# Latent attention with a written order on TensorE: keys and queries projected one head ahead, projections set between the transposition and its use

## The chip, the cores and the metric

One core of a Trainium2 chip runs the program. Its engines are TensorE (PE; its weight loads are listed apart as PEld), VectorE (DVE), ScalarE (ACT), GpSimd (POOL) and SyncE (SP), which in this kernel issues most of the DMAs. The metric is the time on the device of one execution, in microseconds (us); smaller is better. A kernel's time is the median of three runs here.

## The reference

A trunk of two layers over 512 tokens of width 1024. The first layer mixes tokens with a gated linear recurrence (HGRN2), the second with latent attention (MLA). Around each mixer stand two half-step SwiGLU blocks of inner width 2816, and at the end of a layer a gated per-layer embedding. The change touches the attention of the second layer alone:

```python
def _mla_mixer(h, positions, k_nope, k_rope, v, w_dq, q_norm, w_uq, w_out):
    c_q = _rmsnorm(h @ w_dq, q_norm)                      # 512 wide latent query
    q = (c_q @ w_uq).reshape(bsz, seq, B_HEADS, B_NOPE + B_ROPE)
    q_nope, q_rope = jnp.split(q, [B_NOPE], axis=-1)      # 128 and 64 wide, 16 heads
    q_rope = _rope(q_rope, positions)
    ...
        s = (jnp.einsum('bqhd,bkhd->bhqk', qn, k_nope)
             + jnp.einsum('bqhd,bkd->bhqk', qr, k_rope)).astype(jnp.float32) * scale
        s = jnp.where(mask[None, None], s, -jnp.inf)      # causal
        pr = jax.nn.softmax(s, axis=-1).astype(v.dtype)
        return jnp.einsum('bhqk,bkhd->bqhd', pr, v)
    ...
    return o @ w_out
```

`k_nope` and `v` are projected, head by head, from one normalised latent of width 256 that the first layer left; `k_rope` is one rotated key shared by all heads.

## The kernel before

**Numbers in two halves.** Every product is made of three passes in a reduced float type: a tensor is split into a rounded high half and the remainder, and `mm3` multiplies high by high (L151), low by high and high by low into the same accumulation. A split is a copy on ACT (`hi`, L166) and a subtraction on DVE (`lo`, L167). A matmul of `mm3` cannot start before its halves exist, and the second and third passes need the low halves, which come last.

**The stream of weights.** All weights come in one sequence of tiles of 128 by 1024, each eight blocks of 128 by 128, in the order in which TensorE uses them. A tile passes through three stages: a DMA into `raw` (five buffers, issued by SP), a cast on ACT into `whi` (L129, three buffers), a subtraction on DVE into `wlo` (L130, three buffers). The cast of a tile waits until TensorE has done with the tile three places earlier, whose `whi` buffer it takes. `block()` hands out the next block.

**PSUM.** Four banks named `mm` take the projections (`chain`), four named `aux` the scores, the transposed probabilities and the weighted sums.

**The attention**, `mla`, does for each of 16 heads: `scores`, which projects the head's key from the two blocks of the shared latent and its query from the four blocks of the query latent, splits both, and computes four rows of tiles, row i having 128(i+1) columns, then the softmax of each row: masked maximum on DVE (L1142), the scaled negative maximum (L1146), exponential with its sum on ACT (L1149), reciprocal on DVE (L1151), multiplication on POOL (L1152); `weigh`, which transposes the ten tiles of probabilities (L1163), splits the three banks (`ph` on ACT, L1167, and `pl` on DVE, L1168), multiplies by the values and splits the result; and `project`, which multiplies the weighted values of two heads by half of the output weights and adds four results into x (L1182). `rope(group)` makes the rotated queries of four heads: two chains on TensorE, eight operations on ACT and DVE, two splits, and sixteen DMAs (`qr`, L1099) issued by SP. `values(p)` makes the values of two heads. The loop calls scores(h), then weigh(h-1), then for most heads a project; the rope of the next group at h = 3, 7 and 11 and the values of the next pair at odd h.

**Who sets the order.** Outside of stretches under `tc.manual_schedule`, a planner orders the instructions of each engine by a simulated time and by priority; `soon(n)` raises the priority of what is written in it (`FETCH_OFF`, 200, for the stream; `EV_OFF`, 400). Before the change the planner orders every engine in `mla`. In the SwiGLU blocks the order is the written one on all engines. Each engine works through its own list in order: an instruction that waits holds back what stands behind it in the list. The weight stream's tiles are ordered by a list on the host (`_stream`) that has to match the order of use.

Of the kernel before, what the change touches and what calls it, by code (L numbers as in the profile page):

```python
# [9 lines left out]
F32 = mybir.dt.float32  # L10
# [47 lines left out]
def kernel(  # L58
# [1008 lines left out]
    def mla(xg, stats, cn, krope, sin, cos, post):  # L1067
# [13 lines left out]
        def rope(group):  # L1081
            pa, pb = chain(cq), chain(cq)
            qa, qb, ta, tb = (slot("rt") for _ in range(4))
            act.copy(qa, pa)
            act.copy(qb, pb)
            dve.tensor_tensor(out=ta, in0=qa, in1=cos, op=ALU.mult)
            dve.tensor_tensor(out=tb, in0=qb, in1=sin, op=ALU.mult)
            dve.tensor_tensor(out=ta, in0=ta, in1=tb, op=ALU.subtract)
            h1, l1 = split(ta)
            dve.tensor_tensor(out=qb, in0=qb, in1=cos, op=ALU.mult)  # L1090
            dve.tensor_tensor(out=qa, in0=qa, in1=sin, op=ALU.mult)
            dve.tensor_tensor(out=qb, in0=qb, in1=qa, op=ALU.add)
            h2, l2 = split(qb)
            res = []
            for j in range(4):
                d = slot("qr", F32R)
                s = slice(32 * j, 32 * j + 32)
                for i, src in enumerate((h1, h2, l1, l2)):
                    nc.sync.dma_start(d[32 * i : 32 * i + 32, :].bitcast(F32), src[s, :].bitcast(F32))  # L1099
                res.append(d)  # L1100
            return res

        def values(p):
            w = [block(2) for _ in range(2)]
            tiles = []
            for i in range(2):
                pv = mm_bank()
                for n in range(2):
                    j = 2 * i + n
                    for k in range(2):  # L1110
                        ck = tuple(a[:, j * P : (j + 1) * P] for a in cn[k])
                        mm3(pv[:, 256 * n : 256 * n + 256], ck, w[k], k == 0, k == 1)
                tiles.append(split(pv, None, "v"))
            return [
# [5 lines left out]
            ]  # L1120
# [35 lines left out]
        def weigh(prob, v):  # L1156
# [8 lines left out]
            for b, w in ((0, 512), (1, 512), (2, 256)):  # L1165
                hi, lo = slot("ph", F32R, "r"), slot("pl", F32R, "r")
                act.copy(hi[:, 0:w], banks[b][:, 0:w])  # L1167
                dve.tensor_tensor(  # L1168
                    out=lo[:, 0:w], in0=banks[b][:, 0:w], in1=hi[:, 0:w].bitcast(F32), op=ALU.subtract
                )  # L1170
                at.append((hi, lo))
            po = aux_bank()
            for j in range(NT):
                b, o = place[j]
                w = T - j * P
                mm3(po[:, j * P :], v[j], (at[b][0][:, o : o + w], at[b][1][:, o : o + w]), j == 0, j == NT - 1)
            return split(po, None, "o")
# [14 lines left out]
        qr, vals = rope(0), values(0)  # L1192
        last = None
        for h in range(B_HEADS):
            ahead = h < B_HEADS - 1
            rotated, value = qr[h % 4], vals[h % 2]
            if h % 4 == 3 and ahead:
                qr = rope(h // 4 + 1)
            if h % 2 == 1 and ahead:
                vals = values(h // 2 + 1)  # L1200
            pr = scores(rotated)
            if last is not None:
                outs.append(weigh(*last))
            last = (pr, value)
            if 2 < h < B_HEADS - 1:
                project((h - 1) // 2 - 1, 1 - h % 2)
        n = B_HEADS - 1
        half = [mm_bank() for _ in range(KC // 2)]
        for ps in half:
            part(ps, (n - 3, n - 2), True, False)  # L1210
        for ps in half:
            part(ps, (n - 1,), False, False)
        outs.append(weigh(*last))
        for m, ps in enumerate(half):
            part(ps, (n,), False, True)
            add(m, ps)
            post(m)
        for m in range(KC // 2, KC):
            ps = mm_bank()
            part(ps, (n - 3, n - 2, n - 1, n), True, True)  # L1220
            add(m, ps)
            post(m)
# [91 lines left out]
def _stream(i):  # L1314
# [65 lines left out]
    turned(0)  # L1380
    valued(0)
    def project(n, part):
        a, b, c = 2 * n * P, (2 * n + 1) * P, (2 * n + 2) * P
        rows = [wo[a:b], wo[b:c]]
        if n < B_HEADS // 2 - 1:
            rows = rows[::-1]
        out.append(_blocks(np.concatenate(rows, axis=0)[:, part * D // 2 : (part + 1) * D // 2]))

    for h in range(B_HEADS):
        ahead = h < B_HEADS - 1  # L1390
        if h % 4 == 3 and ahead:
            turned(h // 4 + 1)
        if h % 2 == 1 and ahead:
            valued(h // 2 + 1)
        out.append(_blocks(wk[:, h, :128]))
        out.append(_blocks(wq[:, h, :128]))
        if 2 < h < B_HEADS - 1:
            project((h - 1) // 2 - 1, 1 - h % 2)
    tail = wo[-4 * P :]
    out.append(_rows(tail[: 2 * P, : D // 2]).reshape(2, KC // 2, P, P).transpose(1, 0, 2, 3).reshape(-1, P, P))  # L1400
    out.append(_rows(tail[2 * P : 3 * P, : D // 2]))
    out.append(_rows(tail[3 * P :, : D // 2]))
    out.append(_blocks(tail[:, D // 2 :]))
# [67 lines left out]
```

## Time and profile before

| | |
|---|---|
| three runs | 2176.10, 2176.32, 2176.52 us; median 2176.32 us |
| profiled execution, its own time | 2175.48 us |
| its span in the profile | 2173.7 us |
| granted TensorE clock, mean | 0.997 |
| PE busy | 2148.8 us, 99% of the span |
| DVE, ACT, POOL busy | 70%, 45%, 14% |
| attention of the second layer (`mla`, loop and entrance) | about 1447 to 1772 us of the span |

The span is that of the hardware profiler; the time of the execution is 1.8 us longer. A line of a group reads: source line, engine, operation, output and inputs with shapes, count, busy us with the mean of one in ns, and the idle time of the engine just before with what ended it. A line of a timeline reads: start, duration, engine, line, operation, and in brackets the idle time before it and its releaser. Line numbers are those of the kernel before (the changed file's lines are a few higher: L1142 becomes L1148, L1149 becomes L1155, L1163 becomes L1169, L1167 becomes L1174).

### The profile page before, as it was taken

Reading aid. Unit: us, or ns where it says so; the run is one execution under the profiler, and the core shown is the slowest. Engines: PE = TensorE matmul, PEld = TensorE weight load, DVE = VectorE, ACT = ScalarE, POOL = GpSimd, SP = SyncE. Lnnn points to the kernel's source line nnn. Section 1 sums busy time; section 2 is a strip of 40 time slices with the busy share of each in tenths; the row PEclk is TensorE's granted clock in tenths of the full one; section 3 lists DMA queues with packets and bytes.
Section 4 is the critical chain, followed back from the end, with each engine's and each line's share of the span. In section 5 each row is a group of like instructions: output and inputs, shape, how many; then the busy total and the mean of one; then the engine's idle time right before and its main releaser. Section 6 shows DMA issues by size and latency. Waiting matters only on the chain.

```text
span 2173.7 us, 32746 instructions
## 1 busy us (share of the span) xinstructions
PE 2148.8 (99%) x13026; PEld 1925.5 (89%) x13026; DVE 1522.3 (70%) x2261; ACT 968.5 (45%) x1374; POOL 313.3 (14%) x428
## 2 busy tenths in 40 slices
PE   8999999999999999999999999999999999999998
PEld 7899998898888899998888989988888888999987
DVE  6776676777786676675767757767676776775765
ACT  6354453223235343344553525446444563443543
POOL 2000001554521000001110000011110110000011
PEclk9999999999999999999999999999999999999999
DMA  5555552211123555552244655423122134654631
GB/s 192 141 157 159 144 163 96 83 69 59 68 69 105 147 159 159 141 160 101 87 119 127 172 146 157 144 91 104 59 85 91 51 105 132 151 164 126 178 104 49
DMA packets 76249, 261.46 MB, mean 120 GB/s; under 512 B 9152, under 2 KB 11328, under 8 KB 76096
## 3 DMA queue, kind: packets, MB, share of 16 engines
q1 hardware_dynamic: 64864, 220.15, 30.4%
q0 software_dynamic: 10368, 37.75, 10.1%
q8 instruction: 102, 1.67, 0.3%
q10 hardware_dynamic: 864, 1.46, 0.2%
q14 instruction: 51, 0.42, 0.1%
HBM read 253.04 MB, written 2.10 MB: 117 GB/s over the span
## 4 chain that ended last, share of the span: by engine, by line
PE 94%; DVE 3%; ACT 1%; issue 1%; DMA 0%; POOL 0%; SPq 0%; POOLq 0%; DVEq 0%; ACTq 0%
PE aux L314 19%; PE mm L151 18%; PE mm L152 18%; PE mm L153 17%; PE mm L314 14%; PE aux L152 1%; PE aux L153 1%; PE aux L723 1%; PE aux L151 1%; PE aux L1163 1%; PE aux L1138 0%; PE aux L1137 0%; ACT whi L304 0%; PE aux L214 0%; DVE wlo L305 0%
## 5 line engine op out<-in xcount | busy, mean ns | idle before, releaser
L151 PE MATMUL mm<-hi,whi 128*128 128x512 f32 x1656 | 647.1, 393 | 8.5 <-ACT whi L1252 5.6
L152 PE MATMUL mm<-lo,whi 128*128 128x512 f32 x1656 | 647.2, 391 | 1.5 <-DVE lo L380 0.9
L153 PE MATMUL mm<-hi,wlo 128*128 128x512 f32 x1656 | 646.1, 390 | 0.0
L305 DVE TENSOR_TENSOR wlo<-raw,whi 128x1024 fp32r<-128x1024 f32 x340 | 425.3, 1251 | 220.6 <-ACT whi L304 217.5
L304 ACT CAST whi<-raw 128x1024 fp32r<-128x1024 f32 x340 | 355.2, 1046 | 288.3 <-PE mm L152 163.5
L151 PEld LDWEIGHTS mm<-hi,whi 128*128 128x128 f32 x1656 | 311.3, 188 | 72.2 <-ACT whi L1252 5.6
L152 PEld LDWEIGHTS mm<-lo,whi 128*128 128x128 f32 x1656 | 311.7, 188 | 64.1 <-DVE lo L380 2.2
L153 PEld LDWEIGHTS mm<-hi,wlo 128*128 128x128 f32 x1656 | 311.5, 188 | 63.4
L314 PE MATMUL aux<-hi,whi 128*128 128x256 f32 x1152 | 328.1, 285 | 2.5 <-ACT mm L465 2.5
L314 PE MATMUL aux<-hi,wlo 128*128 128x256 f32 x1152 | 326.8, 284 | 0.2 <-DVE wlo L300 0.2
L314 PE MATMUL aux<-lo,whi 128*128 128x256 f32 x1152 | 326.5, 283 | 0.0
L314 PE MATMUL mm<-lo,whi 128*128 128x256 f32 x864 | 244.5, 283 | 0.0
L314 PE MATMUL mm<-hi,whi 128*128 128x256 f32 x864 | 244.5, 283 | 0.0
L314 PE MATMUL mm<-hi,wlo 128*128 128x256 f32 x864 | 244.4, 283 | 0.0
L314 PEld LDWEIGHTS aux<-hi,whi 128*128 128x128 f32 x1152 | 221.6, 192 | 3.3 <-ACT mm L465 2.7
L314 PEld LDWEIGHTS aux<-hi,wlo 128*128 128x128 f32 x1152 | 221.7, 192 | 0.5 <-DVE wlo L300 0.5
L314 PEld LDWEIGHTS aux<-lo,whi 128*128 128x128 f32 x1152 | 221.6, 192 | 0.5
L288 POOL DMA_DIRECT2D raw<-in_wall x72 | 62.8, 872 | 941.1 <-DMA raw<-in_wall 538.5
L129 ACT CAST whi<-raw 128x1024 fp32r<-128x1024 f32 x95 | 99.8, 1051 | 171.7 <-PE mm L152 113.1
L314 PEld LDWEIGHTS mm<-lo,whi 128*128 128x128 f32 x864 | 165.9, 192 | 0.0
L314 PEld LDWEIGHTS mm<-hi,whi 128*128 128x128 f32 x864 | 165.9, 192 | 0.0
L314 PEld LDWEIGHTS mm<-hi,wlo 128*128 128x128 f32 x864 | 165.9, 192 | 0.0
(248 smaller groups left out, 2883.6 us busy)
## 6 DMA issues: line engine op xcount, KB each, us to landing
raw<-in_wall SPq DMA_DIRECT2D x402, 512.0 KB, 3.3
raw<-in_wall POOLq DMA_DIRECT2D x72, 512.0 KB, 5.8
x<-in_xT SPq DMA_DIRECT2D x8, 256.0 KB, 6.8
qr<-hi SPq DMA_DIRECT2D x32, 64.0 KB, 2.0
qr<-lo SPq DMA_DIRECT2D x32, 64.0 KB, 2.0
out_dram<-o SPq DMA_DIRECT2D x8, 256.0 KB, 2.3
p<-in_pT ACTq DMA_DIRECT2D x4, 256.0 KB, 4.4
raw<-in_wall SPq DMA_DIRECT2D x2, 256.0 KB, 3.6
```

The lines of the kernel that those rows point to most:

```text
L129: act.copy(hi[:, s], raw[:, s])
L151: pe.matmul(out, a[0], b[0], start=first, stop=False)
L152: pe.matmul(out, a[0], b[1], start=False, stop=False)
L153: pe.matmul(out, a[1], b[0], start=False, stop=last)
L288: nc.gpsimd.dma_start(self.raw, wall[self.plus], accum_op=ALU.add)
L304: act.copy(hi, self.raw)
L305: dve.tensor_tensor(out=lo, in0=self.raw, in1=hi.bitcast(F32), op=ALU.subtract)
L314: pe.matmul(o, w[u][:, s], b[i][v], start=first and e + i + n == 0, stop=False, skip_group_check=True)
L723: pe.matmul(sc[:, e * 192 : (e + 1) * 192].rearrange("p (i b n) -> p i b n", i=2, n=3 * m), k[:, j * P : (j + 1) * P], q4[:, :, j * nbt : ...
L1163: pe.transpose(banks[b][:, o : o + P], prob[i][:, j * P : (j + 1) * P], ident)
```

## The change

The loop over the heads now stands under `tc.manual_schedule` for TensorE: TensorE does in `mla`'s loop what is written, in the order in which it is written. The other engines are still ordered by the planner. The key and query of head h+1 are projected (`project_in`) after the scores of head h. `weigh` is taken apart into `turn_over`, the ten transpositions and the split of their banks, and `weigh`, the products. For a head in the middle TensorE does: scores(h), weigh(h-1), key(h+1), query(h+1), turn_over(h), then, where they fall due, the rope of a group (after h = 6 and 10), the values of a pair (after even h from 2 to 12), and a half project (h from 2 to 13). At the beginning the key of head 0, half of the first values, the rope of group 0, the rest of the values of two pairs, the query of head 0 and the key of head 1 come before scores(0); at h = 0 the rope of group 1 stands around the transpositions; nothing stands between the transpositions of head 1 and scores(2). At the end the first half of the output columns collects heads 12 to 14 around the transpositions of the last two heads, and a fifth chain, in an `aux` bank, collects heads 12 to 14 after the last weigh. The splits, the rope's operations and the split of the transposed banks get the priority `EV_OFF`. The number of matmuls, transpositions, weight tiles and DMAs stays the same, and so do the instructions of each engine.

```diff
-        def rope(group):
-            pa, pb = chain(cq), chain(cq)
-            qa, qb, ta, tb = (slot("rt") for _ in range(4))
...
+        def rope(res):
+            pa = chain(cq)
+            yield
+            pb = chain(cq)
+            with soon(EV_OFF):
+                qa, qb, ta, tb = (slot("rt") for _ in range(4))
...
-        def scores(qr):
-            pk = chain(cn)
-            kk = split(pk)
-            pq = chain(cq)
-            qq = split(pq)
+        def project_in(rhs):
+            ps = chain(rhs)
+            with soon(EV_OFF):
+                return split(ps)
+
+        def scores(kk, qq, qr):
...
-        def weigh(prob, v):
+        def turn_over(prob):
...
+            with soon(EV_OFF):
+                for b, w in ((0, 512), (1, 512), (2, 256)):
+                    hi, lo = slot("ph", F32R, "r"), slot("pl", F32R, "r")
+                    act.copy(hi[:, 0:w], banks[b][:, 0:w])
...
+                    at.append((hi, lo))
+            return [tuple(a[:, o : o + T - j * P] for a in at[b]) for j, (b, o) in enumerate(place)]
+
+        def weigh(at, v):
             po = aux_bank()
             for j in range(NT):
...
+                mm3(po[:, j * P :], v[j], at[j], j == 0, j == NT - 1)
+            with soon(EV_OFF):
+                outs.append(split(po, None, "o"))
...
-        qr, vals = rope(0), values(0)
-        last = None
-        for h in range(B_HEADS):
...
+        def tails(h):
+            for ps in half:
+                part(ps, (h,), h == n - 3, h == n)
+
+        with tc.manual_schedule(engines={mybir.EngineType.PE}):
+            kq = {0: [project_in(cn)]}
+            val, rot = [], []
+            vg, rg = values(val), rope(rot)
+            next(vg)
+            next(rg)
+            next(rg)
+            next(vg)
+            next(vg)
+            for _ in values(val):
+                pass
+            kq[0].append(project_in(cq))
+            kq[1] = [project_in(cn)]
+            at = None
+            for h in range(B_HEADS):
+                pr = scores(*kq.pop(h), rot[h])
+                if at is not None:
+                    weigh(at, val[h - 1])
+                if h == 0:
+                    rg = rope(rot)
+                    kq[1].append(project_in(cq))
+                    next(rg)
+                elif h < n:
+                    kq[h + 1] = [project_in(cn), project_in(cq)]
+                else:
+                    tails(n - 2)
+                at = turn_over(pr)
+                if h == 0:
+                    next(rg)
+                elif h == n - 1:
+                    half.extend(mm_bank() for _ in range(KC // 2))
+                    tails(n - 3)
+                elif h == n:
+                    tails(n - 1)
+                if h in (6, 10):
+                    for _ in rope(rot):
+                        pass
+                if h % 2 == 0 and 0 < h < n - 2:
+                    for _ in values(val):
+                        pass
+                if 1 < h < n - 1:
+                    project((h - 2) // 2, h % 2)
+            weigh(at, val[n])
+            fifth = aux_bank()
+            part(fifth, (n - 3, n - 2, n - 1), True, False)
...
@@ -1377,30 +1421,47 @@
...
+    for h in range(B_HEADS):
+        if h == 0:
+            query(1)
+            turned(1)
+        elif h < n:
+            key(h + 1)
+            query(h + 1)
...
```

Three places of the lists show what follows for ACT. First, ACT ahead of the first softmax. In the list before, `hi_13935` and `hi_13958` are the splits of the key and the query of head 0:

```order
L166 CAST hi_13857<-rt_13850 128x512
L166 CAST hi_13864<-rt_13849 128x512
L129 CAST whi_14350<-raw_14348 128x1024
L166 CAST hi_13935<-mm_13928 128x512
L166 CAST hi_13958<-mm_13939 128x512
L166 CAST hi_14063<-mm_14056 128x512
L166 CAST hi_14086<-mm_14067 128x512
```

And now, where `hi_13994` is the split of the query of head 0 and `hi_14005` that of the key of head 1:

```order
L129 CAST whi_14133<-raw_14131 128x1024
L166 CAST hi_13977<-mm_13964 128x512
L166 CAST hi_13900<-rt_13885 128x512
L129 CAST whi_14286<-raw_14284 128x1024
L166 CAST hi_13994<-mm_13981 128x512
L166 CAST hi_14005<-mm_13998 128x512
L1155 ACT_TABLE_LOAD
```

The cast `whi_14286`, whose buffer is that of the tile `whi_13943`, last read by the end of the key projection of head 1, now stands directly ahead of the split of the query of head 0.

Second, ACT at head 1 and scores(2), in the list now (`hi_14273` and `hi_14296` split the key and the query of head 2, the `ph` are the banks of head 1's transposed probabilities, the `P` are the exponentials of head 1):

```order
L1155 ACTIVATE P_14191,t_14192<-P_14191,t_14214,t_13814 128x256
L129 CAST whi_14514<-raw_14512 128x1024
L1155 ACTIVATE P_14190,t_14192<-P_14190,t_14228,t_13814 128x384
L1155 ACTIVATE P_14189,t_14192<-P_14189,t_14242,t_13814 128x512
L1174 CAST ph_14313<-aux_14300 128x512
L166 CAST hi_14273<-mm_14266 128x512
L1174 CAST ph_14317<-aux_14301 128x512
L166 CAST hi_14296<-mm_14277 128x512
L1174 CAST ph_14321<-aux_14302 128x256
```

The splits of head 2's key and query stand between the splits of head 1's transposed banks, and the cast of a weight tile stands between the second and third exponential. In the list before, the splits of head 2's key and query stand ahead of all of head 1's exponentials. DVE at the same place, now (`wlo_14515` is the low half of that tile; L1148 is the masked maximum, whose second row reads its result; `pl` and `lo` are the low halves that belong to the `ph` and `hi` above):

```order
L130 TENSOR_TENSOR wlo_14515<-raw_14512,whi_14514 128x1024
L1157 RECIPROCAL t_14232<-t_14192 128x1
L1148 ISA P_14189,t_14241<-aux_14235,cs 128x512
L1148 ISA t_14241 128x1
L1152 TENSOR_SCALAR t_14242<-t_14241,t_13814 128x1
L1157 RECIPROCAL t_14246<-t_14192 128x1
L1175 TENSOR_TENSOR pl_14314<-aux_14300,ph_14313 128x512
L167 TENSOR_TENSOR lo_14274<-mm_14266,hi_14273 128x512
L1175 TENSOR_TENSOR pl_14318<-aux_14301,ph_14317 128x512
L167 TENSOR_TENSOR lo_14297<-mm_14277,hi_14296 128x512
```

The maximum of the last row of head 1 now stands behind the subtraction of the weight tile.

Third, ACT at head 7, after a rope group, now (`hi_15442` splits the weighted values of head 6, `hi_15453` and `hi_15476` the key and the query of head 8):

```order
L1155 ACTIVATE P_15371,t_15372<-P_15371,t_15394,t_13814 128x256
L166 CAST hi_15442<-aux_15429 128x512
L1155 ACTIVATE P_15370,t_15372<-P_15370,t_15408,t_13814 128x384
L129 CAST whi_15675<-raw_15673 128x1024
L166 CAST hi_15453<-mm_15446 128x512
L1155 ACTIVATE P_15369,t_15372<-P_15369,t_15422,t_13814 128x512
L166 CAST hi_15476<-mm_15457 128x512
```

Before, the list has, at head 7's softmax, the two splits of the projected key and query ahead of the first exponential, since scores(7) made them itself:

```order
L166 CAST hi_15277<-mm_15270 128x512
L166 CAST hi_15300<-mm_15281 128x512
L166 CAST hi_15451<-mm_15444 128x512
L129 CAST whi_15666<-raw_15664 128x1024
L166 CAST hi_15474<-mm_15455 128x512
L1149 ACTIVATE P_15305,t_15307<-P_15305,t_15315,t_13814 128x128
L1149 ACTIVATE P_15306,t_15307<-P_15306,t_15329,t_13814 128x256
```

Now the exponentials of head 7 are mixed with the splits of head 8's key and query and with a weight cast. The rows of POOL are the same as before.

More of the change, by code (lines that the diff above doesn't have):

```diff
@@ L1100, in rope, with values @@
                 res.append(d)
[L1101 to L1103 removed]
+            yield
+        def values(res):
             w = [block(2) for _ in range(2)]
@@ L1190, in part @@
                 mm3(ps, block(), outs[h], first and i == 0, last and i == len(heads) - 1)
-        qr, vals = rope(0), values(0)
-        last = None
-        for h in range(B_HEADS):
[L1195 to L1206, printed above, removed]
@@ L1207, in mla @@
-        n = B_HEADS - 1
[L1208 to L1222, printed above, removed]
+        n = B_HEADS - 1
@@ new lines, in mla @@
+        half = []
+        def tails(h):
[46 more added lines that the diff above has]
+            part(fifth, (n - 3, n - 2, n - 1), True, False)
+            for m, ps in enumerate(half):
+                part(ps, (n,), False, True)
+                add(m, ps)
+                post(m)
+            for m in range(KC // 2, KC):
+                if m == KC // 2:
+                    ps = fifth
+                    part(ps, (n,), False, True)
+                else:
+                    ps = mm_bank()
+                    part(ps, (n - 3, n - 2, n - 1, n), True, True)
+                add(m, ps)
+                post(m)
```

87 lines of the change are left out of this document (45 added, 42 removed).

## The prediction

> **What bounds the kernel now.** I began with the page, for the bound, then cut the attention into windows.
>
> ```profile
> span 2173.7 us, 32746 instructions
> PE 2148.8 (99%) x13026; PEld 1925.5 (89%) x13026; DVE 1522.3 (70%) x2261; ACT 968.5 (45%) x1374; POOL 313.3 (14%) x428
> PE 94%; DVE 3%; ACT 1%; issue 1%; DMA 0%; POOL 0%; SPq 0%; POOLq 0%; DVEq 0%; ACTq 0%
> ```
>
> TensorE is busy for 99% of the span and carries 94% of the chain that ended last. The number of matmuls and their widths does not change, so the change can move only TensorE's waits, and only those of the attention. There the windows give (us, then busy time and count of PE, PEld, DVE, ACT, POOL, the granted clock, DMA share, GB/s):
>
> ```profile
> 1447.00:1462.00 15.00, 15.00 (x81) 12.86 (x80) 10.88 (x15) 8.51 (x13) 0.00 (x0) 1.00 0.21 71
> 1462.00:1478.00 16.00, 15.28 (x86) 13.24 (x85) 14.05 (x23) 9.89 (x15) 1.49 (x2) 1.00 0.36 104
> 1500.00:1512.00 12.00, 10.19 (x62) 8.74 (x61) 8.81 (x29) 7.65 (x19) 2.43 (x5) 1.00 0.40 109
> 1512.00:1734.00 222.00, 221.22 (x1201) 190.29 (x1200) 158.21 (x373) 109.34 (x218) 28.64 (x51) 1.00 0.22 72
> 1734.00:1746.00 12.00, 11.25 (x61) 9.30 (x61) 5.68 (x11) 5.14 (x10) 0.71 (x1) 1.00 0.12 44
> 1447.00:1772.00 325.00, 320.93 (x1726) 275.38 (x1725) 237.61 (x532) 172.37 (x329) 43.43 (x72) 1.00 0.24 77
> ```
>
> Over 325 us TensorE idles 325.00 - 320.93 = 4.07 us: 0.72 at the start, 1.81 at 1500 to 1512, 0.78 in 222 us of middle heads, 0.75 at the end. That understates the loss, because a bar is longer than the step to the next start:
>
> ```profile
> 1468.28 0.28 PE L152 MATMUL mm<-wlo,hi 128*128 128x256 f32 x1
> 1468.40 0.28 PE L153 MATMUL mm<-whi,lo 128*128 128x256 f32 x1
> 1469.40 0.50 PE L151 MATMUL mm<-hi,whi 128*128 128x512 f32 x1 [0.72 <-DVE lo L167]
> 1469.97 0.39 PE L153 MATMUL mm<-hi,wlo 128*128 128x512 f32 x1
> 1470.20 0.40 PE L151 MATMUL mm<-hi,whi 128*128 128x512 f32 x1
> ```
>
> Undisturbed, a 256-wide matmul starts 0.12 us after the one before it, a 512-wide one 0.23. The row at 1469.40 came 1.00 after its forerunner, so its 0.72 of idle was 0.88 of lost time. Counted in this way, start to start, the nine stalls of the attention lose 7.7 us (the largest is 1.8, below). This is all that any order can gain: 0.35% of the time.
>
> ```profile
> 1502.71 1.38 PE L1163 MATMUL aux<-cs,P 128*128 128x128 f32 x10
> 1505.61 0.47 PE L151 MATMUL aux<-ph,hi 128*128 128x512 f32 x1 [1.53 <-DVE t L1142]
> ```
>
> Ten transpositions take 1.38 with the last one's bar of 0.27, so 0.11 a step. Between the rows no matmul was in reach and TensorE waited 1.53.
>
> **What a wait costs.** Whether the new order gains depends on how fast ACT, DVE and POOL answer. From the same place, ACT first, then DVE, then POOL:
>
> ```profile
> 1504.58 0.56 ACT L1167 CAST ph<-aux 128x512 fp32r<-128x512 f32 x1
> 1505.05 0.58 ACT L166 CAST hi<-mm 128x512 fp32r<-128x512 f32 x1
> 1506.48 0.84 ACT L1149 ACTIVATE P<-P,t,t 128x512 f32<-128x512 f32 x1
> 1507.19 0.21 ACT L1149 ACTIVATION_READ_ACCUMULATOR P<-P,t,t 128x1 f32 x1
> ```
> ```profile
> 1504.79 0.67 DVE L1142 CUSTOM_DVE_ANT_0 P<-aux,cs 128x512 f32<-128x512 f32 x1
> 1505.99 0.20 DVE L1146 TENSOR_SCALAR t<-t,t 128x1 f32<-128x1 f32 x1
> 1506.71 0.68 DVE L1168 TENSOR_TENSOR pl<-aux,ph 128x512 fp32r<-128x512 f32 x1
> 1507.31 0.68 DVE L167 TENSOR_TENSOR lo<-mm,hi 128x512 fp32r<-128x512 f32 x1
> 1507.90 0.15 DVE L1151 RECIPROCAL t<-t 128x1 f32<-128x1 f32 x1
> ```
> ```profile
> 1508.22 0.69 POOL L1152 TENSOR_SCALAR P<-P,t 128x512 f32<-128x512 f32 x1 [2.67 <-PE aux L153]
> ```
>
> A high half holds ACT 0.47 (start to start), a low half holds DVE 0.60. The softmax of a 512-wide row, with nothing between, is 0.67 + 0.20 + 0.84 + 0.21 + 0.15 + 0.69 = 2.76, with some hand-over 2.9 us from the maximum's start to a tile that can be transposed. The weight stream shares both engines:
>
> ```profile
> L129 ACTq EVENT_SEMAPHORE  x36: 17/136/5722, 1438.4 to 1734.5; - x36
> L129 ACT CAST whi<-raw x36: 1037/1052/1068, 1441.4 to 1735.4; 128x1024 fp32r<-128x1024 f32 x36
> L130 DVE TENSOR_TENSOR wlo<-raw,whi x37: 1207/1224/1227, 1439.6 to 1736.5; 128x1024 fp32r<-128x1024 f32 x37
> ```
>
> A weight cast takes 1.05 and its subtraction 1.22, and the first row is what matters most: ACT stood at such a cast for up to 5.7 us until its buffer came free. What stands behind it in ACT's list stands too. Before, the splits on TensorE's path mostly stood ahead of such a cast.
>
> **The change part by part.** TensorE's list is now fixed, and ACT's and DVE's lists are those that the planner made for it. I walk through them with the durations above. Let z be the time since the end of scores(h). Then weigh ends at z = 1.89 (12 matmuls, three of each width: 3 x 0.63), the key's six 512-wide matmuls at 3.25, the query's twelve at 5.97. Of the transpositions six use rows 0 to 2 (0.65), so row 3 is wanted at z = 6.63. A result can be read some 0.2 after its last matmul's step.
>
> *Removed.* All nine waits of before stand in an order that no longer exists: -7.7.
>
> *Start.* Between rope(0) and scores(0) stand values (to 4.3 us), query 0 (to 7.05) and key 1 (to 8.4). ACT has the cast of `whi_14286` ahead of the query's split, and its buffer is released by the last matmuls of key 1. So ACT waits to 8.4, casts to 9.5, and the split whose input was there at 7.2 is done at 10.0 to 10.2. DVE's subtraction of the tile ends at 10.8, the query's low half at 11.5. SyncE's first rotated queries arrive no sooner:
>
> ```profile
> L1099 SPq DMA_DIRECT2D qr<-hi x32: 507/586/1404, 1469.8 to 1667.0; - x32
> DMA to landing us min/median/max: 1.9/2.0/3.6
> ```
>
> Their low half is ready at 9.3 and lands 2.0 later, at 11.4. The scores are wanted at 8.4: +2.9 (at least 1.6, where the high half alone decides).
>
> *Transpositions of head 1.* The third exponential stands behind the cast of `whi_14514`, whose buffer query 2 releases half-way, at z = 4.6. Cast to 5.7, exponential to 6.5; DVE has the subtraction to 7.0, then the maximum of row 3 to 7.7, its scalar to 8.0, exponential to 8.9, reciprocal, POOL to 9.9. Wanted 6.63: +3.3 (1.9, where the subtraction comes behind the maximum, as at head 7 below).
>
> *scores(2).* Nothing stands between the transpositions and these scores, and ACT splits a bank, the key, a bank, the query: 0.1 + 4 x 0.47 = 2.0; DVE follows in the same order, and its fourth, the low half that the third matmul needs, ends at 0.6 + 4 x 0.6 = 3.0. The third matmul was wanted at 0.2: +2.8 (2.0 if the high halves alone decide).
>
> *Heads 4, 6, 8, 10, 12, 14.* ACT has the split of weigh (to 2.6), the third exponential (to 3.4), the key's split, the fourth exponential; DVE takes the key's low half (4.2 to 4.8) ahead of row 3's scalar, so exponential to 5.9, POOL to 6.95: +0.3 each, +2.0 with rounding up where two splits meet (0 to 2.4).
>
> *Heads 7 and 11.* After a rope group a weight cast stands ahead of the key's split and the fourth exponential: cast 4.6 to 5.7, split 6.2, exponential 7.1; the subtraction of the tile ends at 7.0, the key's low half at 7.6, the reciprocal at 7.75, POOL at 8.5: +1.9 each, 3.8 (1.2 each, without the low half and the subtraction).
>
> *Heads 0, 2, 3, 5, 9, 13.* Row 3 is ready at 5.9 or sooner: 0, hidden under the key and query of the next head. This is what the change does well.
>
> *End.* The transpositions of head 15 are wanted after 5.3 and ready after 5.8, +0.6; the way into the SwiGLU block has one chain less behind the last weigh and waits some 0.5: +1.1 (0 to 2).
>
> The sum is 2.9 + 3.3 + 2.8 + 2.0 + 3.8 + 1.1 = 15.9, less 7.7: +8.2. On the span of 2173.7 that gives 2181.9, and 1.8 more (2175.48 against 2173.7) as time of that execution, 2183.7; the median of before is 0.84 above its profiled execution, so 2184.5. With the low ends, 1.6 + 1.9 + 2.0 + 0 + 2.4 + 0 = 7.9, the change costs nothing. With high ends, where each of the three large gates is 1.2 later by one more subtraction and the rest at the upper bound, it is about 21, +13: 2189.5.
>
> A rule stands beside these sums. The windows above show the clock at 1.00 where TensorE idled for 1.81 us. The Trainium skill ("TensorE: Matmul & The Clock Gate", Part 1) has a free-running window of 3.4 us, after one idle window of which TensorE runs at half clock; by it the stall of 1.81 was harmless, as the trace shows, and the stall of 3.3 at head 1 would be at the edge.
>
> **The rivals.** *All waits go (faster).* The softmax of a head has 6 us of matmuls to hide under, its chain needs 2.9, and weights flow in time: 2176.3 - 7.7 = 2168.6. For it speaks that ACT is busy 172.37 of 325 us and DVE 237.61; against it that the lists put splits behind casts that cannot start, whatever the load. Chance 0.05.
>
> *The gates open earlier (no change).* Buffers are released somewhat sooner than I reckon, or the hand-overs overlap, and the sum is at its low ends: 2176 to 2179. Chance 0.15.
>
> *My forecast*: 2184.5, by itself 2180.5 to 2189. Chance 0.68.
>
> *A late list runs on (slower still).* After the start ACT and DVE do not catch up: with DVE at 14.05 of 16.00 us busy in the window 1462 to 1478, each wait of heads 0 to 2 makes the next operation late, and heads 0 and 2 to 6 wait 0.8 more each: 2184.5 + 6 = 2190.5. Against it, the window of 222 us shows DVE at 71%. Chance 0.09.
>
> *The clock falls.* If the granted clock went to half for as long as each of the three stalls near 3 us had lasted, 9 us more: 2193.5. The 1.81 us at full clock speak against it. By the skill's page it takes an idle window of 3.4 us, which only the stall at head 1 comes near. Chance 0.03.
>
> **How the numbers follow.** A difference of 0.2% (4.4 us) is about what a measurement here tells from no change: faster is below 2172, slower above 2180.7. Faster: the first rival and a little beside it, 0.06. Same: the second rival and the foot of the forecast, 0.17. Slower: 0.77. The range of 8 in 10 takes the forecast, half of the second rival and half of the fourth: 2177.5 to 2190.5; the likeliest case has 2184.5.
>
> **What would show it.** In the changed profile TensorE's rows should idle: before the first score matmul (released by a split or a `qr` DMA), in front of the last four transpositions of heads 1, 7 and 11 (released by POOL), and at the third matmul of scores(2) (released by DVE); heads 3, 5, 9 and 13 should run through. ACT's wait at L129 should end on TensorE at the start and at heads 1, 7, 11. Idle of TensorE in the attention should be around 12 us, where it was 4.07. Wrong would be: no idle at the start or at head 1 (the lists hold nothing back), idle somewhere else, or a clock below 1.00 in the attention.

## The result and the profile after

The changed kernel takes 2188.73 us (five runs, 2187.72 to 2189.43) where the kernel before, on the same chip, takes 2176.39 us: slower by 12.3 us. The ratio is 1.0056, with an interval of 1.0044 to 1.0069. A first set of five gave a median of 2189.49 us; it held two disturbed executions (7883.52 and 11081.1 us), which are left out of its ratio, and the profile read here is from the second set. The profiled execution took 2187.72 us with a span of 2185.9.

The windows of the attention (us, busy time and count of PE, PEld, DVE, ACT, POOL, then the granted clock), in the changed kernel:

```profile
1462.00:1478.00 16.00, 13.62 (x75) 12.16 (x74) 12.86 (x26) 9.99 (x17) 0.85 (x2) 0.89 0.34 93
1500.00:1512.00 12.00, 9.98 (x44) 8.79 (x45) 6.14 (x22) 5.83 (x15) 1.68 (x5) 0.72 0.25 72
1512.00:1734.00 222.00, 217.52 (x1195) 189.30 (x1195) 157.49 (x361) 105.94 (x210) 24.82 (x47) 1.00 0.23 72
1447.00:1784.00 337.00, 323.37 (x1721) 278.72 (x1720) 239.44 (x532) 171.19 (x328) 41.09 (x72) 0.98 0.24 74
```

The attention now lasts some 12 us longer, and TensorE idles 337.00 - 323.37 = 13.63 us in it, against 4.07 in the 325 us of before. In 222 us of middle heads it idles 4.48, where it was 0.78. And two windows have a clock under 1.00, which none had before. What the waits end on (engine and tile, releaser, us in total, times, the longest):

```profile
PE aux L1169 <- POOL P L1158: 8.1, 11, 1.7
PE aux L151 <- ACT hi L166: 2.9, 2, 1.5
PE aux L153 <- DVE lo L167: 1.3, 2, 0.9
```

Eleven waits of transpositions (L1169) for the normalised probabilities, then the splits ahead of two heads' scores. The rows at the start, TensorE first, then ACT:

```profile
1469.89 0.39 PE L153 MATMUL mm<-hi,wlo 128*128 128x512 f32 x1
1471.71 0.33 PE L151 MATMUL aux<-hi,hi 128*128 128x128 f32 x1 [1.44 <-ACT hi L166]
1473.09 0.47 PE L153 MATMUL aux<-hi,lo 128*128 128x128 f32 x1 [0.94 <-DVE lo L167]
```
```profile
1470.13 1.04 ACT L129 CAST whi<-raw 128x1024 fp32r<-128x1024 f32 x1 [2.13 <-PE mm L152]
1471.08 1.06 ACT L166 CAST hi<-mm 128x512 fp32r<-128x512 f32 x2
```

ACT stood 2.13 us at the weight cast until TensorE had done with the key of head 1, and the splits of query 0 and key 1 came only then. At heads 1 and 2, TensorE, ACT, DVE:

```profile
1497.93 0.55 PE L1169 MATMUL aux<-cs,P 128*128 128x128 f32 x3 [1.28 <-POOL P L1158]
1500.15 1.03 PE L1169 MATMUL aux<-cs,P 128*128 128x128 f32 x4 [1.67 <-POOL P L1158]
1502.69 0.47 PE L151 MATMUL aux<-hi,hi 128*128 128x128 f32 x1 [1.50 <-ACT hi L166]
1503.74 0.47 PE L153 MATMUL aux<-hi,lo 128*128 128x128 f32 x1 [0.37 <-DVE lo L167]
```
```profile
1494.82 1.05 ACT L129 CAST whi<-raw 128x1024 fp32r<-128x1024 f32 x1 [1.27 <-issue]
1495.78 0.70 ACT L1155 ACTIVATE P<-P,t,t 128x384 f32<-128x384 f32 x1
...
1500.58 0.59 ACT L1174 CAST ph<-aux 128x512 fp32r<-128x512 f32 x1 [1.54 <-PE aux L1169]
1501.06 0.59 ACT L166 CAST hi<-mm 128x512 fp32r<-128x512 f32 x1
```
```profile
1495.90 1.23 DVE L130 TENSOR_TENSOR wlo<-raw,whi 128x1024 fp32r<-128x1024 f32 x1 [1.32 <-ACT whi L129]
1497.05 0.16 DVE L1157 RECIPROCAL t<-t 128x1 f32<-128x1 f32 x1
1497.12 0.67 DVE L1148 CUSTOM_DVE_ANT_0 P<-aux,cs 128x512 f32<-128x512 f32 x1
```

The row of the weight cast at head 1 names no releaser for its 1.27 us ("issue"); it starts at 1494.82, just behind the matmul half-way through the query of head 2 that the forecast had as the release of its buffer. The third exponential of head 1 comes out from behind this cast, the maximum of its last row from behind the tile's subtraction, and the splits of head 2's key and query are alternated with those of the transposed banks. Head 7, TensorE, then ACT:

```profile
1608.08 0.82 PE L1169 MATMUL aux<-cs,P 128*128 128x128 f32 x6
1610.62 0.66 PE L1169 MATMUL aux<-cs,P 128*128 128x128 f32 x4 [1.73 <-POOL P L1158]
```
```profile
1606.73 1.05 ACT L129 CAST whi<-raw 128x1024 fp32r<-128x1024 f32 x1 [0.29 <-ACT P L1155]
1608.16 0.81 ACT L1155 ACTIVATE P<-P,t,t 128x512 f32<-128x512 f32 x1
```

Here too the last exponential comes out from behind a weight cast and a split.

The fall of the clock is the part that was not in the sum. The clock is at 0.50 in pieces of just 3.41 us, each shown with the piece ahead of it:

```profile
1469.58:1472.99 3.41, 1.13 (x6) 0.53 (x4) 3.08 (x6) 2.84 (x4) 0.00 (x0) 1.00 0.45 123
1472.99:1476.40 3.41, 3.31 (x13) 3.31 (x14) 1.86 (x9) 1.36 (x4) 0.37 (x1) 0.50 0.41 99
1496.88:1500.30 3.42, 0.69 (x4) 0.46 (x5) 1.29 (x6) 0.91 (x2) 1.28 (x2) 1.00 0.45 110
1500.30:1503.71 3.41, 1.57 (x6) 0.98 (x5) 2.51 (x5) 2.33 (x5) 0.00 (x0) 0.50 0.49 115
1503.71:1507.12 3.41, 3.38 (x13) 3.38 (x14) 1.59 (x8) 0.76 (x3) 0.37 (x1) 0.50 0.31 121
```

Two of the three slow pieces are full of matmuls (3.31 and 3.38 us): at half clock some 1.7 us of each is lost, 3.3 together by this estimate.

### The profile page after: what moved, and what is told of

Same layout as the page of the kernel before. It is cut to its first block, busy times and chain, and to the rows that moved or that the text cites. A ratio compares the mean times of both kernels' runs of the same rounds, so it can differ in the third digit from the quotient of the medians.

```text
span 7881.7 us, 32717 instructions
## 1 busy us (share of the span) xinstructions
PE 7865.1 (100%) x13026; PEld 5845.7 (74%) x13026; DVE 1552.9 (20%) x2261; ACT 980.8 (12%) x1374; POOL 295.5 (4%) x428
## 3 DMA queue, kind: packets, MB, share of 16 engines
q8 instruction: 102, 1.67, 0.1%
## 4 chain that ended last, share of the span: by engine, by line
PE 100%; issue 0%; DVE 0%; ACT 0%; DMA 0%; POOLq 0%; POOL 0%; SPq 0%; DVEq 0%; ACTq 0%
PE aux L314 19%; PE mm L151 19%; PE mm L152 18%; PE mm L153 18%; PE mm L314 15%; PE aux L153 2%; PE aux L151 2%; PE aux L152 2%; PE aux L723 2%; PE aux L1169 1%; PE aux L1143 0%; PE aux L1144 0%; PE aux L214 0%; PE aux L222 0%; PE aux L205 0%
## 5 line engine op out<-in xcount | busy, mean ns | idle before, releaser
L151 PE MATMUL mm<-hi,whi 128*128 128x512 f32 (+1 forms) x1652 | 1857.7, 1125 | 5.6 <-ACT whi L1296 5.6
L152 PE MATMUL mm<-lo,whi 128*128 128x512 f32 (+1 forms) x1652 | 1841.2, 1115 | 0.0
L153 PE MATMUL mm<-hi,wlo 128*128 128x512 f32 (+1 forms) x1652 | 1838.9, 1113 | 0.0
L151 PEld LDWEIGHTS mm<-hi,whi 128*128 128x128 f32 x1652 | 789.1, 478 | 573.4 <-issue 562.3
L153 PEld LDWEIGHTS mm<-hi,wlo 128*128 128x128 f32 x1652 | 782.4, 474 | 581.5 <-issue 569.4
L152 PEld LDWEIGHTS mm<-lo,whi 128*128 128x128 f32 x1652 | 793.9, 481 | 559.3 <-issue 557.1
L314 PE MATMUL aux<-hi,whi 128*128 128x256 f32 x1152 | 845.4, 734 | 0.0
L314 PE MATMUL aux<-lo,whi 128*128 128x256 f32 x1152 | 843.5, 732 | 0.0
L314 PEld LDWEIGHTS aux<-lo,whi 128*128 128x128 f32 x1152 | 741.6, 644 | 4.2 <-issue 4.2
L314 PEld LDWEIGHTS aux<-hi,wlo 128*128 128x128 f32 x1152 | 740.5, 643 | 0.1
L314 PEld LDWEIGHTS mm<-hi,wlo 128*128 128x128 f32 x864 | 560.2, 648 | 0.0
L314 PEld LDWEIGHTS mm<-lo,whi 128*128 128x128 f32 x864 | 559.0, 647 | 0.0
L314 PEld LDWEIGHTS mm<-hi,whi 128*128 128x128 f32 x864 | 556.6, 644 | 0.0
```

The source lines that it names most:

```text
L151: pe.matmul(out, a[0], b[0], start=first, stop=False)
L152: pe.matmul(out, a[0], b[1], start=False, stop=False)
L153: pe.matmul(out, a[1], b[0], start=False, stop=last)
L314: pe.matmul(o, w[u][:, s], b[i][v], start=first and e + i + n == 0, stop=False, skip_group_check=True)
```

## The experiments

**The change alone, and the priorities alone.** The first run is the changed kernel once more, for the profile above.

> The changed kernel once more, unaltered, for a profile at full clock. Theory (lists of ACT and DVE hold the splits back): TensorE idles about 12 us in the attention (4.07 before), at the start before the first scores (about 2.9), in front of the last transpositions of head 1 (about 3.3) and of heads 7 and 11 (about 1.9 each), and at the third matmul of scores(2) (about 2.8); heads 3, 5, 9, 13 run through. Time 2184 to 2190 us. Rival (a late list runs on): further idle of 0.8 or so at heads 3 to 6. Rival (the clock): a granted clock under 1.00 in windows of the attention.

Measured: 2188.73 us. The large waits stand where they were forecast, and the clock, the least likely of the rivals, falls too. The second run puts only the priorities of the change into the kernel before:

```diff
         def scores(qr):
             pk = chain(cn)
-            kk = split(pk)
+            with soon(EV_OFF):
+                kk = split(pk)
...
```

> The kernel before with only the priorities of the change: splits, rope operations and the split of the transposed banks carry the raised priority, the order of TensorE stays the planner's. Theory: the priorities are not what costs; the lists change little and the time stays within 0.2% of 2176.4. Rival (the priorities push ACT's and DVE's work into a worse order): several us slower, like the change.

Measured: 2176.32 us against 2176.39, ratio 1.0001 (0.9992 to 1.0010). In the order of before, the priorities alone cost nothing; the loss comes with the new order of TensorE and the lists that the planner makes for it. Whether the planner would make better lists for the new order without these priorities, no run shows.

**What the clock costs.** Idle work is put where TensorE stands still; the aim is that only the clock changes:

```diff
+        def spin(bank, times):
+            for _ in range(times):
+                pe.transpose(bank, ident, ident)
...
-                pr = scores(*kq.pop(h), rot[h])
+                pr = scores(*kq.pop(h), rot[h], {0: 13, 2: 13}.get(h, 0))
...
-                at = turn_over(pr)
+                at = turn_over(pr, (0, 0, 11, 15) if h == 1 else ())
```

> The change, with 52 idle transpositions of the identity matrix added where TensorE stood still: 13 ahead of scores(0), 11 and 15 between the transpositions of head 1, 13 ahead of scores(2), each into a place of a bank that the next matmul overwrites. The waits stay as they are; only TensorE is no longer idle in them. Theory (half a clock after the long idle times is a part of the loss, about 3.2 us: two stretches at 0.50 in the changed profile): the clock stays at 1.00 in the attention and the time falls by about 3, to 2185.5. Rival (the slow stretches are hidden by what other engines owe anyway): clock at 1.00, time unchanged at 2188.7.

Measured: 2185.39 us, 3.3 less than the change, while TensorE does 52 transpositions more. The windows of this run:

```profile
1462.00:1478.00 16.00, 15.05 (x95) 13.42 (x94) 12.86 (x26) 9.89 (x17) 0.93 (x3) 1.00 0.31 84
1500.00:1512.00 12.00, 10.99 (x64) 9.50 (x62) 7.34 (x23) 5.95 (x16) 2.15 (x4) 1.00 0.23 66
```

The clock is at 1.00 in both windows and nothing else is repaired: head 7 still idles its 1.73 us. Of 12.3 us, some 3.3 are the clock and some 9 the waits.

**Cover ahead of scores(2).** The rope of group 2 goes from behind head 6 to behind head 1, with its weights:

```diff
-                if h in (6, 10):
+                if h in (1, 10):
                     for _ in rope(rot):
                         pass
```

> The change, with the rope of group 2 moved from behind the transpositions of head 6 to behind those of head 1; the planner orders the other engines anew. Theory (scores(2) waits because nothing stands ahead of it, and head 7 waits because of the rope before it): the waits ahead of scores(2) go, with half of the slow clock, and the 1.9 us of head 7 goes; head 2 may take over about 1.9: 2182 to 2185. Rival (ACT and DVE are late at head 2 whatever stands there): waits of the same size move to weigh(1) or to the transpositions of head 2, time within 1 us of 2188.7.

Measured: 2188.42 us, the rival's time. The waits moved much as the theory had it: that of head 7 is gone, that ahead of scores(2) too, and head 2 has one of 2.02 where I allowed 1.9. TensorE idles 12.30 us in the 337, where it was 13.63. What the theory missed is the clock: there are again three pieces at half clock, at 1473.57, 1500.88 and, new, at 1521.36 behind the wait of head 2, and TensorE is busy for 3.37 to 3.41 us of each, where one of the change's three was less than half full. At head 2 the rope's operations on DVE and its splits stand between the maxima and exponentials, and a weight cast ahead of the last exponential:

```profile
1520.82 0.66 PE L1169 MATMUL aux<-cs,P 128*128 128x128 f32 x4 [2.02 <-POOL P L1158]
...
1522.12 0.41 PE L152 MATMUL mm<-wlo,hi 128*128 128x256 f32 x1
```

The 256-wide matmul, at half clock, has a bar of 0.41 where it was 0.28. Work moved on TensorE alone takes its companions on ACT and DVE along.

**Written lists on ACT and DVE, first try.** TensorE keeps the order of the change. ACT and DVE are ordered by hand up to head 13: a weight tile is cast only behind a point at which its buffer is free, and the reciprocal of a row comes behind the maximum of the next.

```diff
-        with tc.manual_schedule(engines={mybir.EngineType.PE}):
+        with tc.manual_schedule(engines={E.PE, E.Activation, E.DVE}):
...
+    def flush():
+        while stream.get("due", 0):
+            stream["due"] -= 1
+            fetch()
```

> TensorE in the order of the change, but ACT and DVE in a written order as well up to head 13: a weight tile is cast and subtracted only behind the point at which its buffer is free, exponentials and splits in the order in which their inputs come, the reciprocals one row later, the rope of group 1 finished on ACT and DVE after the weigh of head 0. Theory (the order of TensorE is sound, the lists of ACT and DVE cost the time): the waits of heads 1, 4, 6 to 8, 10 to 12 and most of the start go, scores(2) keeps about 0.9 and the end 1.1; 2171 to 2174, below the kernel before. Rival (the order of TensorE itself leaves too little cover): the time stays at 2184 or more.

Measured: 2188.07 us, as slow as the change, but not for its reasons. No transposition waits any more for POOL, at head 1 or at any second head. In their place stand 2.5 us at the start, two waits of 1.79 for DVE's low half behind the ropes of heads 6 and 10, and one large wait of my own making, at scores(2), with the clock at half for three pieces in and behind it and for one behind the start. The large one, TensorE, then ACT:

```profile
1503.14 0.47 PE L158 MATMUL aux<-hi,hi 128*128 128x128 f32 x1 [4.70 <-ACT hi L173]
```
```profile
1498.20 0.62 ACT L173 CAST hi<-rt 128x512 fp32r<-128x512 f32 x1 [2.68 <-DVE rt L1101]
1501.50 0.62 ACT L173 CAST hi<-rt 128x512 fp32r<-128x512 f32 x1 [2.69 <-DVE rt L1105]
```

I had put the splits of rope 1 ahead of those of head 2's key and query, and ACT stood twice for DVE's rope operations, with what TensorE needed behind it. The same mechanism, in another place. The same lists with the rope of group 2 moved to head 1 as well:

```diff
+            while later:
+                for _ in later.pop(0):
+                    pass
...
+            if h in (1, 10):
+                rg = rope(rot)
```

> The same with the rope of group 2 behind the transpositions of head 1, its operations on ACT and DVE after the weigh of head 1. Theory: the 0.9 us ahead of scores(2) goes too, 2170 to 2173. Rival (the banks and the operations of the rope make head 2 late instead): 1 to 3 us above the run with the lists alone.

Measured: 2182.80 us, between the 2170 to 2173 of the theory and the rival, which had 2189 or more. The cover hides the wait for the splits at scores(2) (1.24 us for a bank stay there), but the start (2.55), head 2 (1.86) and the group after head 10 (1.80) still wait, and two pieces are at half clock.

**A third order.** TensorE's order itself is changed too: more work ahead of scores(0), and a key behind the transpositions of heads 0 and 1, so that something stands ahead of the next scores.

```diff
             kq[0] = [project_in(cn)]
+            kq[1] = [project_in(cn)]
+            run(values(val))
...
+            if h < 2:
+                kq[h + 2] = [project_in(cn)]
+                flush()
```

> A third order, written on TensorE, ACT and DVE: as in the run with the written lists, and besides keys 0 and 1 and the first values ahead of rope 0, the first half of rope 1 ahead of scores(0), its second half and key 2 behind the transpositions of head 0, key 3 behind those of head 1; the eight operations of a later rope on DVE are spread between the additions of the project that follows, not put in one piece. Theory (the waits come from what the lists of ACT and DVE put ahead of a result that TensorE needs, plus too little cover ahead of scores(0) and scores(2)): no wait over 0.4 us in heads 1 to 13, the start under 1.5, the end 1.0; the clock at 1.00; 2170 to 2174, below the kernel before. Rival (the order of TensorE with keys and queries ahead is itself too tight, since each head needs more of DVE than it hides): waits of 1 to 2 us remain at heads with values or a rope, 2177 or more.

Measured: 2189.74 us. The start has no wait over 0.81, heads 0 and 1 and scores(2) none over 0.49, but three waits of 3.6 to 3.7 us have come, at the weigh after scores(3), (7) and (11). TensorE, then DVE at the first:

```profile
1521.67 0.77 PE L158 MATMUL aux<-ph,hi 128*128 128x512 f32 x1 [3.66 <-DVE t L1170]
```
```profile
1518.06 0.69 DVE L1108 TENSOR_TENSOR rt<-rt,sin 128x512 f32<-128x512 f32 x1
1518.66 0.68 DVE L1213 TENSOR_TENSOR x<-mm,x 128x512 f32<-128x512 f32 x1
1519.26 0.68 DVE L1110 TENSOR_TENSOR rt<-rt,rt 128x512 f32<-128x512 f32 x1
1520.63 0.69 DVE L174 TENSOR_TENSOR lo<-rt,hi 128x512 fp32r<-128x512 f32 x1 [0.68 <-ACT hi L173]
1521.23 0.28 DVE L1170 CUSTOM_DVE_ANT_0 P<-aux,cs 128x128 f32<-128x128 f32 x1
```

The four score rows had filled the four `aux` banks, the weigh needs one of them, and the maximum that frees the first (L1170) stands on DVE behind the tail of the rope's operations. So the rope is spread thinner, and at the start, not among the lines below, a weight tile is cast in the middle of rope 0's operations instead of behind them:

```diff
                 for g in later:
                     next(g, None)
-                    next(g, None)
-            while later:
-                run(later.pop())
...
+            if h > 2:
+                while later:
+                    run(later.pop())
```

> The third order with the operations of a later rope spread thinner on DVE: one behind each of the four additions of the project and the other four behind the weigh of the next head; at the start a weight tile is cast between the third and fourth operation of rope 0, where it stood behind all of them. Theory (the three waits of 3.6 to 3.9 us of the third order, each for the maximum of a first row, come from the rope's operations that stand ahead of it on DVE, and the wait at 1471 from the late cast): these waits and the half clock after them go, 10.8 us of wait and about 4 of clock; 2172 to 2176. Rival (DVE has more work than time at a head with a rope, wherever its pieces stand): two or three waits of 1 to 3 us come back one head later, 2179 or more.

Measured: 2173.88 us against 2176.23, ratio 0.9988 (0.9979 to 0.9997): faster than the kernel before by 2.35 us. The largest of the waits that are left:

```profile
PE aux L158 <- DVE t L1170: 1.3, 3, 0.5
PE aux L221 <- DVE sq L195: 0.8, 1, 0.8
PE aux L158 <- DVE pl L1197: 0.5, 1, 0.5
```

TensorE's idle time in the 337 us is 3.73, as its window shows:

```profile
1447.00:1784.00 337.00, 333.27 (x1791) 287.95 (x1790) 246.62 (x543) 178.82 (x340) 44.09 (x75) 1.00 0.26 80
```

Sixteen microseconds lie between the two last runs, and only the places of a few operations on DVE and ACT differ. Ten of them are idle time (13.71 against 3.73 in the same window); the rest goes with the clock, which was at half for four pieces in the third order and for none here.

**Two orders by two kinds of lists.** To tell the lists from the order of TensorE, the order of the change gets the lists that spread the rope (first lines), and the third order the lists that the planner makes (last two lines):

```diff
-            kq[1] = [project_in(cn)]
-            run(values(val))
+            vg = values(val)
+            next(vg)
...
-        with tc.manual_schedule(engines={E.PE, E.Activation, E.DVE}):
+        with tc.manual_schedule(engines={mybir.EngineType.PE}):
```

> TensorE in the order of the change; ACT and DVE in the written lists of the run that spreads the rope's operations (one behind each addition of the project, the rest behind the weigh of the next head). With the change itself (2188.7), the third order with the same lists (2173.9) and the third order with the planner's lists it makes a table of two orders by two kinds of lists. Theory (the lists are most of the loss, the order of TensorE a small part): the waits at the transpositions of heads 1, 4, 6 to 8, 10 to 12 and 14 go, as does the wait for the splits ahead of scores(2), where 0.9 remains for the banks; the start keeps 1 to 3 us: 2174 to 2179. Rival (the order of TensorE is most of the loss): 2183 or more.

> TensorE in the third order (keys 0 and 1 and the first values ahead of rope 0, half of rope 1 ahead of scores(0), key 2 behind the transpositions of head 0, key 3 behind those of head 1); ACT and DVE in lists that the planner makes, with the priorities of the change. Theory (the lists are most of the loss): waits of 1 to 3 us at heads 1, 7 and 11 and of 0.4 at every second head stay, as in the change: 2182 to 2188. Rival (the order of TensorE is most of the loss): under 2178.

Measured: 2178.78 us (ratio 1.0011, 1.0002 to 1.0020) and 2185.68 us (1.0045, 1.0031 to 1.0058).

| order of TensorE | lists of the planner | written lists |
|---|---|---|
| the change's | 2188.73 | 2178.78 |
| the third | 2185.68 | 2173.88 |

Beside each of the four the kernel before took 2176.2 to 2176.4. These lists are worth 9.9 us in the one order and 11.8 in the other; the order of TensorE 3.0 and 4.9. That the lists are written is not enough: the first written lists gave 2188.07 in the order of the change, and 2189.74 in the third. And by the profiles the 3.0 is the clock rather than the waits: in that of the third order with the planner's lists TensorE idles 337.00 - 323.27 = 13.73 us, as much as the 13.63 of the change, but no piece is at half clock:

```profile
1447.00:1784.00 337.00, 323.27 (x1738) 278.25 (x1737) 240.02 (x532) 174.00 (x331) 41.66 (x72) 1.00 0.24 74
```

In the third order with the planner's lists the waits of the change are back, with the planner's signature:

```profile
1500.81 0.66 PE L1169 MATMUL aux<-cs,P 128*128 128x128 f32 x4 [1.67 <-POOL P L1158]
...
1608.53 0.66 PE L1169 MATMUL aux<-cs,P 128*128 128x128 f32 x4 [1.73 <-POOL P L1158]
```

In the order of the change with written lists, the start and the banks at scores(2) remain, and both still bring a piece at half clock. TensorE is busy for 3.41 us of each, so by the same estimate they are 3.4 of the 4.9:

```profile
1471.20 0.33 PE L158 MATMUL aux<-hi,hi 128*128 128x128 f32 x1 [0.84 <-ACT hi L173]
1472.99 0.33 PE L160 MATMUL aux<-hi,lo 128*128 128x128 f32 x1 [1.35 <-DVE lo L174]
...
1499.83 0.39 PE L158 MATMUL aux<-hi,hi 128*128 128x256 f32 x1 [1.46 <-DVE pl L1197]
```

## Why the prediction was right, and where it was not

The forecast was 2184.5 us within 2177.5 to 2190.5, slower; measured were 2188.73 and 2189.49. The direction, the places of the waits and their mechanism were right, and the time fell into the upper part of the range. With the clock held at 1.00 the change took 2185.39, 0.9 from the forecast: that is the fair test of the sum. That 2188.73 still lies inside is in part luck, since the upper end came from a rival that did not come (a late list that runs on) and not from the clock. One of the prediction's own signs of being wrong, a clock below 1.00 in the attention, did come. Point by point, in time lost from start to start, the longer step of the first matmul behind a wait included:

| step | forecast | measured |
|---|---|---|
| start, scores(0) | 2.9 | 2.7 |
| transpositions of head 1 | 3.3 | 3.3 |
| scores(2), third matmul | 2.8 | 2.9 |
| heads 4, 6, ..., 14 | 2.0 | 2.5 (each idles 0.20 or 0.21) |
| heads 7 and 11 | 3.8 | 3.9 (each idles 1.73) |
| heads 0, 2, 3, 5, 9, 13 | 0 | 0 |
| end | 1.1 | 1.7 (0.7 and 1.0) |
| entrance, ahead of rope 0 | not in the sum | 1.0 |
| the clock | not in the sum | 3.3 |

At scores(2) the longer wait (1.50) is that of the first matmul for ACT's split, and the third, which the prediction named, waits 0.37 more for DVE. At heads 7 and 11 the weight cast idles only 0.29, and its row names ACT's exponential where the prediction said TensorE. The start is right for half of its reason. ACT and DVE released it, as the lists said. The rotated queries, which I had reckoned to arrive at the same time, hold nothing back in these rows: the matmul that uses them comes 0.27 after the third. With cover ahead of scores(0) they do come last, by 0.45 us (the run that spreads the rope) to 1.18 (the third order with the planner's lists).

The sum of the waits by this table is 18.0, less the 7.7 of before 10.3; the run with the idle time filled gives 9.0, and the idle time itself grew by 9.6 (13.63 less 4.07). The 1.3 between them is not settled; some of the rows at scores(0) and scores(2) were taken while the matmuls ran at half clock, so that a part is counted twice. The 7.7 is uncertain too: counted strictly, as gaps between starts that are 0.15 us or more over the undisturbed step, the stalls of before come to 6.4 in its trace.

The step that failed is the price of the clock, which stood at zero in the sum and at 0.03 among the rivals. The argument was that TensorE had idled 1.81 us at full clock before, and that no idle time but that of head 1 would come near 3.4. But the 1.81 was the sum over a window of 12 us, with 1.53 in its longest gap. The runs showed that the idle time need not be in one piece: no gap at the start was over 1.44 us and none at head 1 over 1.67, and the clock fell all the same, after pieces of 3.41 us in which TensorE was busy 1.13 and 0.69. The 9 us of that rival were too much, since the slow pieces are 3.41 us long and not all full: 3.3. The rule of the Trainium skill that the prediction cited ("TensorE: Matmul & The Clock Gate", Part 1) agrees in the length of the window and in its running free: the edges at 1472.99 and 1500.30 lie 27.31 us apart, eight times 3.41. Read as a rule about one unbroken gap of 3.4 us, it does not agree.

The entrance was left out because my walk began at the end of rope 0. There the second rope chain's ancestor, the fourth latent query, is split while the rope already wants it; the row of that wait names ACT's split (L169), 0.56 of idle.

The rival in which all waits go (2168.6) did not come, and no run reached it: the same order of TensorE is 9.9 us better with other lists, but still 2.6 above the kernel before, and the best run has 2173.88. The rival of a late list that runs on did not come: heads 3, 5, 9 and 13 show no wait.

## What to carry to other kernels

Where one engine's order is fixed by hand, the lists of the engines that feed it decide: read, for each result that the engine waits for, what stands ahead of it in its producer's list, and whether that can start. Here the same order of TensorE gave 2188.7, 2188.1 or 2178.8 us with three kinds of lists, and a few operations moved by a few microseconds on DVE and ACT were worth up to 16. And add up idle time over a stretch of some 3.4 us, not gap by gap, before a clock is taken for granted.

## What the runs showed of the hardware

TensorE's granted clock fell to 0.50 for whole pieces of 3.41 us on a fixed grid, after pieces in which TensorE was busy 0.20 and 0.33 of the time (the change), and in the order of the change with written lists even after one with 0.56:

```profile
1497.69:1501.11 3.42, 1.90 (x12) 1.76 (x13) 3.14 (x9) 1.48 (x4) 0.00 (x0) 1.00 0.26 66
1501.11:1504.52 3.41, 3.41 (x10) 2.84 (x9) 1.88 (x10) 2.08 (x6) 0.85 (x2) 0.50 0.24 93
```

In the third order with the planner's lists, waits of 1.10 and 1.18 in a row, and of 1.24 and 1.67, left the clock at 1.00. The change itself has such a case, at head 11, ahead of a piece at full clock:

```profile
1684.61:1688.02 3.41, 1.68 (x13) 1.27 (x12) 2.48 (x4) 2.02 (x5) 0.69 (x1) 1.00 0.59 153
```

So it counts where the idle time falls on the grid. In the profiles of this case's attention, pieces at full clock with TensorE busy 0.45 or less were all followed by half clock, and none with 0.57 or more; between these both occur (after 1.62 us busy of 3.42 the clock fell in the run with the lists and the rope, after 1.63 of 3.42 it held in that with the first written lists). Where in there the line lies is open, the more so as the ends of matmuls are modelled. The 52 idle transpositions were enough to hold the clock.
